# Earlier columns, later vectors, a later fourth block: the input stage of an encoder layer

## The chip, the cores and the metric

One core of one Trainium2 chip runs the whole layer in one launch. The metric is the device time in microseconds (us) of an execution; the time before is the median of three runs. Engines are named as in the profile: PE is TensorE, DVE VectorE, ACT ScalarE, POOL GpSimd, and SP the SyncE queue, from which nearly all transfers are issued.

## The reference

The input x has 2048 tokens of 1024 features. One layer is computed:

```python
h = rms_norm(x, norm_mix)
z = h @ w_in            # 1024 x 4352: q_A k_A v_A q_B k_B v_B gate_A gate_B
y_a = windowed_gqa(q_a, k_a, v_a, sink)     # window of 128 to both sides, ALiBi, a sink logit per head
y_b = neighborhood_attn(q_b, k_b, v_b, rpb) # 8 x 16 neighbourhood on a 32 x 64 grid
merged = sigmoid(g_a) * (y_a @ w_proj_a) + sigmoid(g_b) * (y_b @ w_proj_b)
x = x + merged @ w_out
x = x + relu(rms_norm(x) @ w_up)**2 @ w_down
return rms_norm(x)
```

The change lies in the product `h @ w_in`, in its first some 365 of 2631 us.

## The kernel before

**Precision.** Every fp32 operand of a matmul is split into a high part (a rounded copy, ScalarE, L293 or L176) and a low part (source minus high, VectorE, L294 or L177). One product is three matmuls: high x high, high x low, low x high (L297 to L299, and L200 to L202 in feature tiles).

**Blocks of x.** The tokens form four blocks of 512. Blocks 0 and 1 are loaded as four tiles of 128 tokens each (`x_tiles`, L365), normalised on VectorE, turned on PE (`turned`, L287, into a PSUM bank), and evicted with the gain `g_mix` by ScalarE (`scaled`, L517) and VectorE (`scaled_less`, L520). Blocks 2 and 3 are loaded later, normalised on ScalarE (`normalised`, L236), turned in 32 x 32 pieces on VectorE (`turned_out`, L260) and written to a tensor `h1d` in device memory (L268, 16 writes a block); `h_pages` (L678, split in L681 and L682) reads them back in the attention stage.

**Groups of columns ("quads").** For blocks 0 and 1, `in_quad` multiplies a 2 x 2 arrangement of halves (two halves of the features, two sets of columns; two blocks) in seven products instead of eight, in this order:

```python
ORDER = (1, 2, 5, 6, 7, 4, 3)
QUADS = [(O_KA, P), (O_QA, 256), (O_QB, 256), (O_KB, 256), (O_VB, 256)]
QUADS += [(O_GA + n * BT, 256) for n in range(4)]
```

Products 1 and 2 use only block 0 and the first set of columns of w_in: rows 0 to 511 for product 1, 512 to 1023 for product 2. The later ones use sums and differences of the halves, on the weights' side made by `in_left` (L290), on the tokens' side written out by hand between the `next(...)` calls. Results leave PSUM through L497 (ScalarE), L290, L439, L442/L443 and go to device memory by L463 and L474.

`row_half` (L527) loads one half of the rows with both sets of columns of a quad: 512 KB of K/V weights (`kvw`) for quad 0, 1 MB (`zraw`) for quad 1. Quads 0 and 1 run interleaved; the first two products of quad 2, whose first columns come by L571, are put ahead of quad 0's and 1's fifth. Each x tile of block 1 can be turned only when it is normalised (L222, L224, L227, L228, L557).

**Groups 2 to 8.** The loop over `q` runs quads 2 to 8, and loads each quad's weights one quad ahead. In q = 5 and q = 6 it also loads, normalises and turns blocks 2 and 3. In q = 7 the bias tables are made.

**Attention.** It starts when the quads end. The score matmuls are L758/L759, score reduction L760 (VectorE), softmax L763 to L771, transposes of the weights L777, products with v L782/L783. Between them "feature tiles" (`qk_tile`, `v_tile`, `gate_tile`) compute h @ w_in for blocks 2 and 3 from the h1d pages; their weight slices are loaded by L187 and split in L176/L177.

**What sets the order.** The program is traced in the order written. A scheduler in the language's tile layer then places every engine's instructions by its own timeline and by priorities, within the dependencies and the rings of buffers; each engine then runs its own list strictly in order. SP too: its issue of a transfer waits for what the transfer needs, and for the landing of the transfer eight earlier. `tc.issue_after(x)` keeps an instruction behind x.

Of the kernel before, what the change touches and what calls it, by code (L numbers as in the profile page):

```python
# [18 lines left out]
AH = 8  # L19
# [3 lines left out]
P = 128  # L23
KC = D // P
NB = 4
BT = 512
# [66 lines left out]
def encoder_layer(ctx, tc, x, norm_mix, w_in, b_gate, sink, rpb, w_pa, w_pb, w_out,  # L93
                  norm_mlp, w_up, w_down, norm_final, dist_a, mask_b, out):
    nc = tc.nc
    V, A, G, PE, SY = nc.vector, nc.scalar, nc.gpsimd, nc.tensor, nc.sync
# [9 lines left out]
    def pools(stack, side, tags, name):  # L106

        return {t: pool(f"{name}_{t}", side=side, stack=stack) for t in tags}
# [15 lines left out]
    def T(pl, shape, dt, tag, bufs):  # L124
        n_t[0] += 1
        pl = pl[tag] if isinstance(pl, dict) else pl
        return pl.tile(shape, dt, tag=tag, bufs=bufs, name=f"{tag}_{n_t[0]}")
# [5 lines left out]
    bg = cp.tile([P, 24], F32, name="bg")  # L133
    sink_t = cp.tile([P, AH], F32, name="sink_t")
# [11 lines left out]
    def bcast(ap1d, n):  # L146
        return bass.AP(ap1d.tensor, ap1d.offset, [[0, P], [1, n]])
# [9 lines left out]
    h1d = [dp.tile([D, BT], F32, name=f"h1d{b}") for b in range(2)]  # L157
# [53 lines left out]
    last_dma = [None]  # L211

    def load_tile(pl, tag, bufs, rows):
        t = T(pl, [P, D], F32, tag, bufs)
        last_dma[0] = SY.dma_start(t, rows).ins
        return t
# [14 lines left out]
    def rstd_of(pl, t, jp=None, mean=False):  # L231

        st = T(pl, [P, 4], F32, "st", 4)
        junk = T(pl if jp is None else jp, [P, 512], F32, "junk", 1)
        for n in range(2):
            A.activation(junk, t[:, n * 512 : (n + 1) * 512], AF.Square, scale=float(D) ** -0.5 if mean else 1.0,  # L236
                         accum_out=st[:, n : n + 1])
        r = st[:, 2 : 3]
        V.scalar_tensor_tensor(out=r, in0=st[:, 0:1], scalar=EPS if mean else D * EPS, in1=st[:, 1:2],
                               op0=ALU.add, op1=ALU.add)  # L240
        G.tensor_tensor(out=r, in0=r, in1=power, op=ALU.pow)
        return r

    def normalised(pl, tiles, jp=None, by_scalar=False):

        for t in tiles:
            if by_scalar:
                A.activation(t, t, AF.Copy, scale=rstd_of(pl, t, jp, True))
            else:
                V.tensor_scalar(t, t, rstd_of(pl, t, jp), float(D) ** 0.5, ALU.mult, ALU.mult)  # L250

    def turned_out(d, ht, tiles, g, gain=None, queue=None):

        hv = ht.rearrange("p (j t c) -> p t j c", j=8, t=4)
        for t in range(4):
            V.transpose(out=hv[:, t], in_=tiles[t][:, g * 256 : (g + 1) * 256].rearrange("p (j c) -> p j c", j=8))  # L260
        h3 = ht.rearrange("p (j x) -> p j x", j=8)
        if gain is not None:
            (step, n), _ = gain.ap
            gv = bass.AP(gain.tensor, gain.offset + 8 * g, [[step, n], [1, 8], [0, P]])
            V.tensor_tensor(out=h3, in0=h3, in1=gv, op=ALU.mult)
        dv = d.rearrange("(j i) (a x) -> a i j x", i=32, a=4)
        for a in range(4):
            (queue or SY).dma_start(dv[a][:, 8 * g : 8 * g + 8], h3[32 * a : 32 * a + 32])  # L268
# [20 lines left out]
    def add(eng, out, a, b, op=ALU.add):  # L289
        return eng.tensor_tensor(out=out, in0=a, in1=b, op=op).ins  # L290
# [10 lines left out]
    def halves(t):  # L301

        return t[:, 0:2], t[:, 2:4]

    def ring(stack, tag, shape, dt, bufs, side="right"):

        pl = pool(f"r_{tag}", side=side, stack=stack)
        return lambda: T(pl, shape, dt, tag, bufs)
# [22 lines left out]
    in_raw = ring(s_z, "zraw", PAGE, F32, 4, "left")  # L331
# [6 lines left out]
    in_e = ring(s_z, "ze", [P, 2, BT], F32, 2)  # L338
# [3 lines left out]
    kvw = ring(s_kv, "kvw", [P, 4, 256], F32, 2)  # L342
# [11 lines left out]
    def x_tiles(pl, b, bufs):  # L354
        out = []
        for t in range(4):
            xt = T(pl, [P, D], F32, "xin", bufs) if t < bufs else in_v2[0]()
            if b > 1:

                for a in range(4):  # L360
                    r = b * BT + a * P + t * 32
                    SY.dma_start(xt[32 * a : 32 * a + 32], xf[r : r + 32])
            else:
                r = b * BT + t * P
                last_dma[0] = SY.dma_start(xt, xf[r : r + P]).ins  # L365
            out.append(xt)
        return out
# [3 lines left out]
    def in_weights(c, w):  # L371

        return [row_half(c, w, p) for p in range(2)]

    def left_parts(src, w, eng):
        hl = in_whl()[:, :, :, 0:w]
        last_part[0] = split(src, hl[:, 0], hl[:, 1], eng)
        return hl
# [143 lines left out]
    QUADS = [(O_KA, P), (O_QA, 256), (O_QB, 256), (O_KB, 256), (O_VB, 256)]  # L522
    QUADS += [(O_GA + n * BT, 256) for n in range(4)]

    def row_half(c, w, p):
        t = kvw() if w == P else in_raw()
        SY.dma_start(t, w_in[0][p * BT : (p + 1) * BT, c : c + 2 * w].rearrange("(k p) f -> p k f", p=P))  # L527
        return t

    tiles = [x_tiles(xp, 0, 8), None]  # L530
    with nc.allow_non_contiguous_dma(reason="small per-feature vectors"):
        SY.dma_start(g_mix, norm_mix[0].rearrange("(k p) -> p k", p=P))
    ws0 = [row_half(*QUADS[0], p) for p in range(2)]
    ws1 = [row_half(*QUADS[1], 0)]
    tiles[1] = x_tiles(xp, 1, 8)
    ws1.append(row_half(*QUADS[1], 1))
    with tc.issue_after(last_dma[0]), nc.allow_non_contiguous_dma(reason="small per-feature vectors"):
        SY.dma_start(bg[:, 0:16], b_gate[0].rearrange("(k p) -> p k", p=P))
        SY.dma_start(sink_t, bcast(sink[0], AH))
    for t in tiles[0]:  # L540
        V.tensor_scalar(t, t, rstd_shared(xp, t), float(D) ** 0.5, ALU.mult, ALU.mult)
    right = {n: (in_page[n](), in_page[n]()) for n in (1, 2)}
# [25 lines left out]
    for p in range(2):  # L568
        t = T(xp, [P, D], F32, "xin", 8).rearrange("p (k c) -> p k c", k=4)
        c = QUADS[2][0]  # L570
        SY.dma_start(t, w_in[0][p * BT : (p + 1) * BT, c : c + 256].rearrange("(k p) f -> p k f", p=P))  # L571
        ops2.append(left_parts(t, 256, V))
        if p == 0:
            with tc.issue_after(last_part[0]):
                for o, h, l in zip(halves(t1), *map(halves, right[1])):
                    add(V, o, h.bitcast(F32), l.bitcast(F32))
        next(quad2)
    for n in (5, 3, 6):
        right[n] = (in_page[n](), in_page[n]())

# [41 lines left out]
    ws = in_weights(*QUADS[2])  # L622

    def bias_tables():
        rp = rpb[0]
        for n, (w, lo_rel) in enumerate(((24, -8), (32, -8), (24, -15))):
            tb = in_e()[0:BH].rearrange("h a b -> h (a b)")[:, 0 : T_ROWS * w]
            tb3 = tb.rearrange("h (r w) -> h r w", w=w)
            G.memset(tb, 0.0)
            ncol = min(w, 15 - lo_rel + 1)  # L630
            first = 15 + lo_rel
            SY.dma_start(tb3[:, T_RO - 7 : T_RO + 8, 0:ncol], rp[:, :, first : first + ncol])

            G.tensor_scalar(tb, tb, 8.0, 1.0, ALU.mult, ALU.mult)
            SY.dma_start(tabs[n], tb)

    for q in range(2, len(QUADS)):
        if q == 5:
            s_v.close()
            in_v2.pop()  # L640
            xp = pools(s_z, "right", ("xin", "st"), "x2")
        if q == 7:
            bias_tables()
        lf = list(in_left(ws, 256, (1, 2) if q == 2 else ()))
        if q + 1 < len(QUADS):
            ws = in_weights(*QUADS[q + 1])
        if q in (5, 6):

            b = q - 3
            xt = x_tiles(xp, b, 3)  # L650
            normalised(xp, xt, Junk(), by_scalar=True)
        ops2.extend(lf if q == 2 else ())
        for n, _ in enumerate(quad2 if q == 2 else in_quad(*QUADS[q], iter(lf), right)):
            if q in (5, 6) and 2 <= n < 6:
                turned_out(h1d[b - 2], in_e().rearrange("p k x -> p (k x)"), xt, n - 2)
    s_z.close()
    s_zp.close()

# [434 lines left out]
    def up_weights(q):  # L1093
        ws = []
        for p in range(2):
            w = up_rings["raw"]()
            SY.dma_start(w, w_up[0][p * BT : (p + 1) * BT, q * BT : (q + 1) * BT].rearrange("(k p) f -> p k f", p=P))
            ws.append(w)
        return ws
# [215 lines left out]
    for b in range(NB):  # L1315
# [43 lines left out]
        for t in range(4):  # L1359
            row0 = b * BT + t * P  # L1360
            xt = load_tile(p4x, "xr", 5, xf[row0 : row0 + P])
# [25 lines left out]
    for m in range(2):  # L1387
# [4 lines left out]
        ws = None  # L1392
        for q in range(8):
# [8 lines left out]
            if q < 7:  # L1402
                ws = up_weights(q + 1)
# [125 lines left out]
    for n in (1, 6, 2, 7, 5, 3, 4):  # L1529
        for group in ((range(8),) if n != 4 else (range(4), range(4, 8))):  # L1530
            part = None if n != 4 else group[0] // 4
# [63 lines left out]
```

## Time and profile before

| | us |
|---|---|
| Runs | 2630.62, 2633.14, 2633.35 (median 2633.14) |
| Profiled execution | 2632.52 |
| Its span on the core | 2630.6 |
| PE busy in it | 2588.6 (98%) |
| Mean granted PE clock | 0.997 of full |
| Quads end, first score matmul | 364.86 after the span's start |

A row of the timeline has the start and the length in us, the engine, the source line, the operation, what it writes and reads, and in brackets how long the engine sat idle before it and what ended that. A waits row names who waited, for which line of which engine, the us in total, how often and the longest. A groups row has busy us and mean ns of one, and the idle time before. A windows row has the stretch, its length, the busy us of PE, PEld (weight load), DVE, ACT and POOL, the granted clock, the DMA engines' share and GB/s. A row of the DMA view gives packets, MB and GB/s of its stretch.

### The profile page before, as it was taken

The numbers are of one execution on the slowest core, as the hardware profiler recorded it, in microseconds if no ns is written. First come the engines' busy times: TensorE is split into PE (matmuls) and PEld (weight loads), VectorE is DVE, ScalarE is ACT, GpSimd is POOL, SyncE is SP. The second block draws the span as 40 slices with busy tenths as digits, with TensorE's granted clock in tenths as the row PEclk, the third lists the DMA queues.
The fourth block names the chain that finished last, engine by engine and source line by source line (L and its number), as shares of the span: only waits on it lengthen the run. The fifth ranks groups of instructions, "written<-read, shape, count | busy, mean of one in ns | idle before, by whom it ended". The sixth has DMA issues, their size and how long they took to land.

```text
span 2630.6 us, 34485 instructions
## 1 busy us (share of the span) xinstructions
PE 2588.6 (98%) x12140; PEld 2154.3 (82%) x12140; DVE 1633.5 (62%) x2661; ACT 1230.6 (47%) x2245; POOL 349.9 (13%) x431
## 2 busy tenths in 40 slices
PE   7999999999999999999999999999999999999998
PEld 6888788778888888888887888888888888888887
DVE  8875666665544444756578677766656634554767
ACT  5334256666555555633334444644544322323444
POOL 1000014344555541000001000000000000000011
PEclk9999999999999999999999999999999999999999
DMA  5657476455876655954556755854428825444554
GB/s 168 204 164 200 133 238 167 113 155 145 241 218 180 189 149 163 311 183 152 170 184 200 244 203 198 306 183 155 145 107 295 302 101 183 146 146 168 184 190 170
DMA packets 352941, 490.28 MB, mean 186 GB/s; under 512 B 27752, under 2 KB 187624, under 8 KB 350592
## 3 DMA queue, kind: packets, MB, share of 16 engines
q1 hardware_dynamic: 345856, 471.30, 56.5%
q10 hardware_dynamic: 6912, 16.78, 1.8%
q8 instruction: 96, 1.57, 0.2%
q14 instruction: 77, 0.63, 0.1%
HBM read 328.53 MB, written 159.45 MB: 186 GB/s over the span
## 4 chain that ended last, share of the span: by engine, by line
PE 89%; DVE 5%; DMA 3%; ACT 2%; issue 1%; SPq 1%; POOL 0%; DVEq 0%; POOLq 0%; ACTq 0%
PE b L297 15%; PE b L299 15%; PE b L298 15%; PE mm L200 6%; PE mm L202 6%; PE mm L201 6%; PE zb L297 3%; PE zb L299 3%; PE zb L298 2%; PE pt L200 2%; PE pt L201 2%; PE pt L202 2%; PE av L960 2%; PE pt L948 2%; PE s L920 2%; PE pt L777 1%
## 5 line engine op out<-in xcount | busy, mean ns | idle before, releaser
L298 PE MATMUL b<-dwh,dah 128*128 128x512 f32 x896 | 349.0, 389 | 0.0
L299 PE MATMUL b<-dwh,dah 128*128 128x512 f32 x896 | 348.2, 390 | 0.0
L297 PE MATMUL b<-dwh,dah 128*128 128x512 f32 x896 | 339.9, 389 | 0.0
L293 ACT CAST dah<-da 128x1024 fp32r<-128x1024 f32 (+1 forms) x128 | 120.9, 945 | 367.7 <-PE b L299 242.7
L294 DVE TENSOR_TENSOR dah<-da,dah 128x1024 fp32r<-128x1024 f32 (+1 forms) x128 | 139.3, 1089 | 224.8 <-ACT dah L293 220.4
L297 PE MATMUL b<-ubh,uwhlb 128*128 128x512 f32 x592 | 230.9, 390 | 5.1 <-ACT uc L1255 3.2
L298 PE MATMUL b<-ubh,uwhlb 128*128 128x512 f32 x592 | 230.6, 390 | 0.0
L299 PE MATMUL b<-ubh,uwhlb 128*128 128x512 f32 x592 | 229.6, 390 | 0.0
L200 PE MATMUL mm<-hT,whl 128*128 128x512 f32 x544 | 218.3, 401 | 0.0
L202 PE MATMUL mm<-hT,whl 128*128 128x512 f32 x544 | 215.4, 396 | 0.0
L201 PE MATMUL mm<-hT,whl 128*128 128x512 f32 x544 | 214.1, 394 | 0.0
L297 PE MATMUL zb<-zh,zwhl 128*128 128x512 f32 x476 | 188.8, 398 | 8.8 <-DVE zc L290 3.7
L299 PEld LDWEIGHTS b<-dwh,dah 128*128 128x128 f32 x896 | 168.4, 188 | 34.8
L298 PEld LDWEIGHTS b<-dwh,dah 128*128 128x128 f32 x896 | 168.4, 188 | 34.7
L297 PEld LDWEIGHTS b<-dwh,dah 128*128 128x128 f32 x896 | 168.3, 188 | 34.7
L298 PE MATMUL zb<-zh,zwhl 128*128 128x512 f32 x476 | 187.7, 394 | 0.0
L299 PE MATMUL zb<-zh,zwhl 128*128 128x512 f32 x476 | 184.1, 394 | 0.3 <-DVE zwhl L294 0.3
L290 DVE TENSOR_TENSOR uc<-b,uc 128x512 f32<-128x512 f32 x160 | 109.1, 688 | 105.1 <-PE b L299 98.0
L1484 POOL TENSOR_TENSOR st<-st,power 128x1 f32<-128x1 f32 x16 | 13.5, 857 | 934.5 <-DVE st L1483 934.3
L297 PEld LDWEIGHTS b<-ubh,uwhlb 128*128 128x128 f32 x592 | 111.2, 188 | 30.0 <-ACT uc L1255 4.1
L298 PEld LDWEIGHTS b<-ubh,uwhlb 128*128 128x128 f32 x592 | 111.2, 188 | 23.0
L299 PEld LDWEIGHTS b<-ubh,uwhlb 128*128 128x128 f32 x592 | 111.2, 188 | 22.9
(248 smaller groups left out, 5902.7 us busy)
## 6 DMA issues: line engine op xcount, KB each, us to landing
at<-uc SPq DMA_DIRECT2D x224, 256.0 KB
da<-at SPq DMA_DIRECT2D x96, 512.0 KB
dw<-in_w_down_dram SPq DMA_DIRECT2D x160, 256.0 KB
uraw<-in_w_up_dram SPq DMA_DIRECT2D x32, 1024.0 KB
raw<-in_w_in_dram SPq DMA_DIRECT2D x34, 512.0 KB
zraw<-in_w_in_dram SPq DMA_DIRECT2D x16, 1024.0 KB
z<-zg SPq DMA_DIRECT2D x64, 256.0 KB
qa<-qs_a SPq DMA_DIRECT2D x32, 256.0 KB
```

The source lines that it names most:

```text
L200: PE.matmul(ps, lh, rh, start=first, stop=False)
L201: PE.matmul(ps, lh, rl, start=False, stop=False)
L202: PE.matmul(ps, ll, rh, start=False, stop=last)
L290: return eng.tensor_tensor(out=out, in0=a, in1=b, op=op).ins
L293: A.copy(hi, src)
L294: return eng.tensor_tensor(out=lo, in0=src, in1=hi.bitcast(F32), op=ALU.subtract).ins
L297: PE.matmul(ps, lh, rh, start=first, stop=False, skip_group_check=True)
L298: PE.matmul(ps, lh, rl, start=False, stop=False, skip_group_check=True)
L299: PE.matmul(ps, ll, rh, start=False, stop=last, skip_group_check=True)
L920: PE.matmul(ps[:, :n], q[:, i, :], kv[:, z, B_R0[i] // 4 : (B_R0[i] + B_NR[i]) // 4, 4 * B_C0[j] : 4 * (B_C0[j] + w)], start=z == 0, stop= ...
L948: PE.transpose(pt[:kp, at + (i - i0) * P : at + (i - i0 + 1) * P], s[i][:, rr : rr + kp], ident)
L960: last = PE.matmul(po[:, i0 * P : (i0 + ni) * P], v[:kp, c, :], src[:kp, o : o + ni * P], start=first, stop=(c == 7 and z == 1), skip_grou ...
```

## The change

- The loads of quads 0 and 1 are cut by columns. All four loads of the first set of columns (needed by products 1 and 2) are issued first, then block 1 of x, then the four loads of the second set, into the other halves of the same tiles. Rows of 512 B and 1 KB take the place of 1 KB and 2 KB.
- The small vectors `bg` (gate bias) and `sink_t` are issued behind quad 2's first products in the program's text.
- Block 3 of x (the fourth) is loaded in q = 7 instead of q = 6, and normalised and turned in q = 8, the last, around products 1 to 4 of the loop's count.

```diff
-    def row_half(c, w, p):
-        t = kvw() if w == P else in_raw()
-        SY.dma_start(t, w_in[0][p * BT : (p + 1) * BT, c : c + 2 * w].rearrange("(k p) f -> p k f", p=P))
+    def row_half(c, w, p, t=None, part=None):
+        if t is None:
+            t = kvw() if w == P else in_raw()
+        use = slice(0, 2 * w) if part is None else slice(part * w, part * w + w)
+        src = w_in[0][p * BT : (p + 1) * BT, c : c + 2 * w]
+        SY.dma_start(t[:, :, use], src[:, use].rearrange("(k p) f -> p k f", p=P))
         return t
...
-    ws0 = [row_half(*QUADS[0], p) for p in range(2)]
-    ws1 = [row_half(*QUADS[1], 0)]
+
+    ws0, ws1 = ([row_half(*QUADS[n], p, part=0) for p in range(2)] for n in range(2))
     tiles[1] = x_tiles(xp, 1, 8)
-    ws1.append(row_half(*QUADS[1], 1))
-    with tc.issue_after(last_dma[0]), nc.allow_non_contiguous_dma(reason="small per-feature vectors"):
-        SY.dma_start(bg[:, 0:16], b_gate[0].rearrange("(k p) -> p k", p=P))
-        SY.dma_start(sink_t, bcast(sink[0], AH))
...
         next(quad2)
+    for n, ws in ((0, ws0), (1, ws1)):
+        for p in range(2):
+            row_half(*QUADS[n], p, ws[p], 1)
+    with tc.issue_after(last_dma[0]), nc.allow_non_contiguous_dma(reason="small per-feature vectors"):
+        SY.dma_start(bg[:, 0:16], b_gate[0].rearrange("(k p) -> p k", p=P))
+        SY.dma_start(sink_t, bcast(sink[0], AH))
...
-        if q in (5, 6):
-
-            b = q - 3
+        if q in (5, 7):
+            b = 2 + q // 7
             xt = x_tiles(xp, b, 3)
+        if q in (5, 8):
             normalised(xp, xt, Junk(), by_scalar=True)
         ops2.extend(lf if q == 2 else ())
         for n, _ in enumerate(quad2 if q == 2 else in_quad(*QUADS[q], iter(lf), right)):
-            if q in (5, 6) and 2 <= n < 6:
-                turned_out(h1d[b - 2], in_e().rearrange("p k x -> p (k x)"), xt, n - 2)
+            if q == 5 and 2 <= n < 6 or q == 8 and 1 <= n < 5:
+                turned_out(h1d[b - 2], in_e().rearrange("p k x -> p (k x)"), xt, n - (2 if q == 5 else 1))
```

## The prediction

> **What bounds the kernel now.** I read the page first (busy time, chain), then PE's waits, then windows around the waits, then the timeline of the places that the change touches.
>
> ```profile
> span 2630.6 us, 34485 instructions
> PE 2588.6 (98%) x12140; PEld 2154.3 (82%) x12140; DVE 1633.5 (62%) x2661; ACT 1230.6 (47%) x2245; POOL 349.9 (13%) x431
> PE 89%; DVE 5%; DMA 3%; ACT 2%; issue 1%; SPq 1%; POOL 0%; DVEq 0%; POOLq 0%; ACTq 0%
> ...
> PE zb L297 <- DVE ze L443: 2.9, 1, 2.9
> PE zb L297 <- DVE zh L520: 2.0, 1, 2.0
> ...
> PE zb L297 <- DVE zc L290: 3.2, 2, 2.3
> ```
>
> TensorE (PE) is busy for 2588.6 of 2630.6 us and carries 89% of the chain, so only 42.0 us of idle time exist, and the change alters no matmul. The time moves by PE's idle time, and by its clock. Three stalls lie in the stages touched: one waits for L443 (2.9 us), one for L520 (2.0), one for L290 (2.3). The next rows show what follows each: window, its length, busy time of PE, PEld, DVE, ACT and POOL, granted clock, DMA share, GB/s.
>
> ```profile
> 24.44:27.85 3.41, 0.99 (x5) 0.49 (x3) 3.41 (x6) 1.23 (x3) 0.00 (x0) 1.00 0.89 291
> 27.85:31.27 3.42, 2.98 (x7) 2.41 (x8) 3.42 (x7) 0.61 (x1) 0.84 (x1) 0.50 0.51 115
> 55.16:58.57 3.41, 1.42 (x7) 0.90 (x6) 3.41 (x6) 2.00 (x2) 0.00 (x0) 1.00 0.00 0
> 58.57:61.98 3.41, 3.41 (x10) 2.65 (x9) 3.41 (x6) 0.00 (x0) 0.00 (x0) 0.50 0.34 67
> 270.20:273.61 3.41, 3.41 (x9) 2.65 (x9) 3.31 (x5) 0.00 (x0) 0.00 (x0) 0.50 0.94 330
> 300.00:340.00 40.00, 40.00 (x178) 33.17 (x177) 18.77 (x22) 11.98 (x15) 0.00 (x0) 1.00 0.25 92
> 1454.50:1457.90 3.40, 1.78 (x9) 1.25 (x8) 2.46 (x4) 2.02 (x3) 0.00 (x0) 1.00 0.97 337
> 1457.90:1461.30 3.40, 3.40 (x17) 2.82 (x16) 0.41 (x1) 1.23 (x2) 0.00 (x0) 1.00 0.94 356
> ```
>
> After a window in which PE was busy for 0.99 or 1.42 of 3.41 us, the next 3.41 us ran at clock 0.50; after one with 1.78 of 3.40 they did not. So each of the three stalls also costs about half of 3.41 us of full-speed work, call it 1.6. What could be gained at most is 2.9 + 2.0 + 2.3 + 3 x 1.6 = 12.0 us.
>
> **Part 1: columns of the first two products first, small vectors later.** The rows of the timeline: start, duration, engine, line.
>
> ```profile
> 12.76 10.25 SPq L539 DMA_DIRECT2D sink_t<-in_sink_dram  x1
> 23.52 1.23 DVE L290 TENSOR_TENSOR zS<-zraw,zraw 128x1024 f32<-128x1024 f32 x1 [2.12 <-DMA zraw<-in_w_in_dram]
> 24.66 0.68 DVE L224 CUSTOM_DVE_ANT_0 ze<-xin 128x512 f32<-128x512 f32 x1
> 25.04 0.39 PE L299 MATMUL zb<-zh,zwhl 128*128 128x512 f32 x1
> 25.46 0.60 ACT L442 ACTIVATE ze<-zb 128x512 fp32r<-128x512 f32 x1 [0.83 <-PE zb L299]
> 27.55 0.68 DVE L443 SCALAR_TENSOR_TENSOR ze<-zb,ze 128x512 fp32r<-128x512 f32 x1
> 28.29 0.79 PE L297 MATMUL zb<-zh,zwhl 128*128 128x512 f32 x1 [2.86 <-DVE ze L443]
> 39.27 1.80 PE L287 MATMUL zb<-ident,xin 128*128 128x128 f32 x15
> 57.10 0.74 DVE L520 SCALAR_TENSOR_TENSOR zh<-zb,g_mix,zh 128x512 fp32r<-128x512 f32 x1
> 57.99 0.47 PE L297 MATMUL zb<-zh,zwhl 128*128 128x512 f32 x1 [1.99 <-DVE zh L520]
> DMA packets 830, 1.12 MB, mean 374 GB/s; under 512 B 24, under 2 KB 539, under 8 KB 830
> DMA packets 702, 2.00 MB, mean 401 GB/s; under 512 B 49, under 2 KB 49, under 8 KB 702
> DMA packets 2072, 1.03 MB, mean 345 GB/s; under 512 B 125, under 2 KB 2048, under 8 KB 2072
> ```
>
> In the changed build the bytes are the same, but 1 MB of w_in moves in rows of 512 B instead of 1 KB and 2 MB in rows of 1 KB instead of 2 KB. The three DMA rows are stretches of 3, 5 and 3 us whose packets are mostly 1 KB and 2 KB, 4 KB, and 512 B. 1 MB at 345 instead of 374 GB/s costs about 0.2 us; 2 MB at 374 instead of some 388 (between 374 and 401) about 0.3. So the last piece lands 0.5 us later: zS (L290) can start at 24.0, not 23.52. The Trainium skill ("DMA: Bandwidth & Descriptors", Why small descriptors are slow) speaks against such a split: a fixed overhead of about 3 cycles a packet beside 32 B a cycle. By it I estimate 0.2 and 0.2 us, and a sum lower by 0.1; the 345 of the trace, 14% under 401, agrees with its 15 to 20% for 512 B.
>
> What is gained: the order on VectorE (DVE) becomes zS, L224, L443, while before an L294 and an L290 (start to start 1.14 us each, 23.52 to 24.66) stood between. zS 24.0 to 25.15, L224 to 25.8, then L443 waits for ACT's L442, which ends at 26.06 as before; with about 0.2 for the hand-over PE goes on at 27.0 instead of 28.29. Its last matmul before the gap still starts near 25.04, since block 0's x and turning are not moved. Gap 1.6 instead of 2.86; the window 24.44:27.85 is then busy for 1.8 of 3.41 us, just as the one that kept its clock. Minus 1.3, and probably minus 1.6.
>
> What is lost: PE's list is rearranged. Before, 15 of block 1's transposes ran together at 39.27. In the build, x tiles 2 and 3 of block 1 each come behind another 12 matmuls. From 27.0: 24 matmuls at 0.225 (178 in the 40.00 us from 300 to 340) and one bank wait of 0.7 give 33.1; 12 matmuls, 12 transposes (0.1 each), 12, 6, 12, 6 bring the last transposes of tile 3 to 43.7. VectorE must then do 16 of L520 (0.66 start to start), four 1024-wide operations (1.14) and three 512-wide ones (0.6): 16.9 us, from 44.9 to 61.8. Before, the last L520 began at 57.10. PE waits for that at its next-to-last step: between 43.7 and 62.0 it has 51 matmuls and 8 transposes, 12.4 us, so 6 us are idle against 1.99; but at 62.0 it stands 15 matmuls (3.4 us) further in its list than at 57.99 before. To a common point 60 matmuls behind 57.99: before 13.6 + 1.6 (half clock) gives 73.2; after, 45 matmuls give 72.2, and VectorE's ten operations ahead of the L290 that frees the bank (nine of 1.14, one of 0.6, then 0.7) hold it to 73.5, or 73.8 with a half clock. Part 1: plus 0.6; if the first stall still halves the clock, plus 2.2; if ScalarE and the scheduler's gaps are kinder, minus 1. Both ends stay in the range. Moving bg and sink costs nothing on PE: their landings are first needed in the attention stage, while sink's issue (10.25 us on SP) still stands ahead of quad 2's loads, as before; these land some 0.5 us later too, and PE needs what is made of them only at 37 us.
>
> **Part 2: block 3 loaded in group 7, turned in group 8.**
>
> ```profile
> 268.01 0.43 DVE L260 STREAM_TRANSPOSE ze<-xin 128x256 f32<-128x256 f32 x1
> 269.50 0.47 PE L297 MATMUL zb<-zh,zwhl 128*128 128x512 f32 x1 [2.32 <-DVE zc L290]
> 348.38 1.05 ACT L176 CAST whl<-raw 128x1024 fp32r<-128x1024 f32 x1 [1.72 <-DMA raw<-in_w_in_dram]
> 349.46 1.23 DVE L177 TENSOR_TENSOR whl<-raw,whl 128x1024 fp32r<-128x1024 f32 x1 [0.86 <-ACT whl L176]
> 364.86 0.28 PE L758 MATMUL s<-ka,qa 128*128 128x256 f32 x1
> 365.58 0.40 PE L200 MATMUL mm<-hT,whl 128*128 128x512 f32 x1
> 365.06 0.69 DVE L290 TENSOR_TENSOR zc<-zb,zc 128x512 f32<-128x512 f32 x1 [1.83 <-PE zb L299]
> L760 DVE CUSTOM_DVE_ANT_0 sa<-s,biasa,sink_t 128x384 f32<-128x384 f32 x26 | 15.2, 606 | 2.4 <-PE s L759 2.3
> L760 DVE CUSTOM_DVE_ANT_0 sa<-s,biasa,sink_t 128x256 f32<-128x256 f32 x8 | 3.7, 480 | 4.4 <-PE s L759 3.8 <-PE pt L777 0.4
> L682 DVE SCALAR_TENSOR_TENSOR hT<-raw,g_mix,hT 128x512 fp32r<-128x512 f32 x8 | 5.6, 747 | 1.8 <-ACT hT L681 1.8
> 366.00:390.00 24.00, 24.00 (x124) 20.65 (x124) 13.39 (x45) 12.95 (x39) 11.61 (x20) 1.00 0.85 254
> PE s L758 <- DVE sta L760: 1.9, 3, 1.1
> PE av L783 <- DVE pl L781: 1.4, 3, 0.8
> ```
>
> Gone: in group 6 the turning (L260) stands ahead of the L290 for which PE waits 2.32 us, and the half clock behind it: minus 3.9. In group 8 the same 16 transposes (0.4 each) fall into a stretch where VectorE is less than half busy (18.77 of 40.00 us from 300 to 340); 0 to 1.5, taken 0.5. Loading and ScalarE's normalising of the four x tiles go along into groups 7 and 8, where ScalarE has 11.98 of 40.00 us and the DMA engines a share of 0.25: nothing, as long as the rows are there a group ahead.
>
> New: the quads end at T (364.86 before). There the weight slice of the first feature tile had long been split (L176 at 348.38, L177 at 349.46), so feature-tile matmuls (L200) at once filled the time in which the softmax of the first attention tiles ran, and PE had 24.00 busy of 24.00 us. In the build SP gets 16 writes of block 3 to h1d ahead of the reads of block 2 (L678) and of the first slice; each of SP's issues waits for the landing of the one eight earlier. The slice's load is issued only near T - 0.4, its cast on ScalarE stands behind the first softmax (to about T + 8.6), and L177 on VectorE stands behind 12 score reductions (L760). Price on VectorE from T: last L290 0.8 (365.06 to 365.7), four L760 of 256 columns 2.4 (0.48 and the reading of the accumulator, taken as 0.59), eight of 384 columns at 0.61, 4.9, small ones 0.6, two L682 at 0.66 back to back, 1.3, L177 1.1, hand-over 0.2: PE's first product with the low half starts at T + 11.3. Until then it has 12 pairs of score matmuls (three pairs of 256 columns fill 364.86 to 365.58, 0.24 a pair, so 0.36 for 384 columns: 4 x 0.24 + 8 x 0.36 = 3.8), two feature-tile matmuls (0.5) and six transposes (0.6): 4.9. Idle 6.4; with 0.7 a reduction, small operations between them, 7.1; taken 6.7. At 40% busy the clock halves as in the rows above: plus 1.6 behind it. Block 3's rows are read through the same ring still later: 0 to 2, taken 0.7.
>
> Part 2: -3.9 + 0.5 + 6.7 + 1.6 + 0.7 = +5.6. Behind that, PE's list is the same as before.
>
> **Sum.** +0.6 + 5.6 = +6.2 on the profiled execution's 2632.52 us (span 2630.6, 1.92 around it) is 2638.7. That execution lies 0.6 below the median of 2633.14, so on the median I forecast 2639. Own range: part 1 from -1 to +2.2, part 2 from +3 (0 in group 8, 6.0 idle, half a half clock, 0) to +7.5: 2635 to 2643.
>
> **The rivals.**
> - Front-loading is repaid. Place: the attention stage from 366 to 620, where PE waits for L760 and L781, 1.9 + 1.4 us. While PE idles at T, twelve reductions are already done, so these waits may vanish: 2639 - 3.3, about 2636, no change. It decides if VectorE keeps that lead for over 100 us; against it speaks that the list behind the first slice is unchanged and each wait is local to a pair.
> - Both stages work as drawn: the slice is not late (its load and cast go out ahead of the softmax), and the second stall of part 1 is hidden: -3.9 - 2.9 - 1 = 2625. The positions in the lists speak against it: 12 L760 ahead of one L177.
> - Worse: the turning in group 8 stalls PE as it did in group 6 (+3.4 more, 3.9 instead of 0.5) and the first stall halves the clock (+1.6): 2644. For it: VectorE is in order, and its L260 waits for a ring of two tiles.
> - A gap under 3 us costs only itself: PE's idle time at T comes in pieces of under 3 us, so no half clock follows, and 1.6 goes from the sum: 2637.4, no change. Against it: the three rows at 0.50 above, behind gaps of 2.86, 1.99 and 2.32 us. The Trainium skill has it as a rule ("TensorE: Matmul & The Clock Gate", Why this matters for your kernels: no idle gaps over some 3 us); this trace disagrees.
>
> **How the numbers follow.** Forecast 0.57, the rule on gaps 0.03, worse 0.16, repaid 0.11, as drawn 0.13. 0.2% (5.3 us) is about what a measurement can tell here: faster is below 2627.9, slower above 2638.4. Of the forecast's own range some 0.65 lies above 2638.4: 0.37, with worse 0.53; its rest, the rule on gaps and repaid make same, 0.34; faster is 0.13. For 8 in 10 I leave out "as drawn" and little else: from "repaid" at the forecast's lower end (2635 - 3.3), less 1.4 (half of what the runs before differ by), 2630, to "worse" with block 3's reading at its upper bound, 2646.
>
> **What would show it.** Right: PE's wait at L443 near 1.6 us; a wait of several us at 50 to 62 us for L520; no wait near 267; in the first 12 us after the quads PE busy near 40%, with waits for L767 (L760 moved) and then for L177, and clock 0.50 behind. Wrong: PE busy over 80% there, or a gap near 27 as long as before.

## The result, and the profile after

| | before | after |
|---|---|---|
| Median of six runs, us | 2632.71 | 2649.18 (2647.78 to 2652.19) |
| Ratio after/before | | 1.0064, 95% interval 1.0054 to 1.0074 |
| First profiled execution, us (span) | 2632.52 (2630.6) | 2652.19 (2650.3) |
| Second profiled execution of the changed kernel, us (span) | | 2648.44 (2646.5) |

The change makes the kernel slower by 16.5 us by the medians, 0.64% by the ratio. Slower was the likeliest sign in the prediction, but the size is outside its range (2630 to 2646).

The first profile happens to be of the longest of the six runs: it has a stall of 2.4 us and a half clock at 118 us that no other profile here shows. So a second profile of the same kernel (**after_again** below) is read here. First its page: span, busy time.

```profile
span 2646.5 us, 34476 instructions
PE 2595.1 (98%) x12140; PEld 2156.6 (81%) x12140; DVE 1634.7 (62%) x2661; ACT 1229.8 (46%) x2245; POOL 358.9 (14%) x431
```

The matmuls are the same 12140. PE's idle time is 51.4 us (2646.5 - 2595.1) against 42.0, and its busy time grew by 6.5 us (2588.6 to 2595.1), in part because of the half clock: matmuls start every 0.43 us there (381 to 383 us) instead of every 0.23 (362 us). PE's waits from 0 to 130 us, then from 360 to 450:

```profile
...
PE zb L297 <- DVE zh L520: 3.1, 1, 3.1
PE zb L297 <- DVE ze L443: 1.5, 1, 1.5
PE zb L297 <- DVE ze L439: 1.2, 1, 1.2
PE zb L297 <- ACT zh L293: 1.0, 1, 1.0
...
PE s L765 <- DVE zc L290: 5.5, 1, 5.5
PE pt L784 <- POOL sa L778: 2.1, 1, 2.1
PE av L789 <- DVE ya L794: 1.9, 1, 1.9
PE mm L200 <- ACT whl L176: 1.1, 1, 1.1
```

The wait for L443 shrank from 2.9 to 1.5, as forecast, and the group-6 wait for L290 is gone (from 255 to 300 us PE waits for nothing). The big new one is the first score matmul (L765, L758 before): 5.5 us. The row names L290, but that ended at 368.0, and q's transfer says more: SP issued it at 359.66 and its last packet landed at 368.71; PE went on at 368.80. In the kernel before, the same transfer took as long (issued at 354.09, landed at 363.03), but that was 1.8 us before PE needed it. The windows show what the clock did (columns as in the prediction):

```profile
59.67:63.08 3.41, 1.18 (x4) 0.48 (x3) 3.41 (x6) 2.12 (x3) 0.00 (x0) 1.00 0.00 0
63.08:66.49 3.41, 1.55 (x4) 1.30 (x5) 3.41 (x5) 1.99 (x2) 0.00 (x0) 0.50 0.02 5
66.49:69.91 3.42, 3.42 (x10) 2.68 (x9) 3.42 (x4) 0.00 (x0) 0.00 (x0) 0.50 0.00 0
363.46:366.87 3.41, 0.00 (x0) 0.00 (x0) 3.15 (x5) 1.63 (x3) 2.50 (x4) 1.00 1.04 330
366.87:370.28 3.41, 1.48 (x7) 1.38 (x7) 1.72 (x5) 0.00 (x0) 0.00 (x0) 0.50 1.14 330
370.28:373.70 3.42, 3.42 (x12) 3.42 (x12) 3.20 (x14) 1.94 (x9) 0.00 (x0) 0.50 1.10 370
373.70:377.11 3.41, 2.36 (x10) 1.28 (x9) 3.41 (x12) 3.41 (x10) 0.00 (x0) 1.00 1.13 232
377.11:380.52 3.41, 1.23 (x7) 0.59 (x7) 2.52 (x8) 2.09 (x8) 3.02 (x4) 1.00 1.14 238
380.52:383.94 3.42, 3.42 (x10) 2.75 (x10) 1.36 (x1) 2.44 (x6) 3.42 (x6) 0.50 1.15 319
438.55:441.96 3.41, 1.49 (x7) 0.87 (x6) 3.41 (x7) 3.39 (x11) 1.56 (x1) 1.00 1.00 331
441.96:445.38 3.42, 3.42 (x13) 3.08 (x13) 2.35 (x9) 1.79 (x7) 0.90 (x2) 0.50 0.93 276
```

Of these windows, each with PE busy for 0.00 to 1.55 of 3.41 us is followed by one at 0.50, and the one with 2.36 by one at 1.00. The half clock is paid three times behind the quads, where the prediction counted it once. Why q came late is in SP's rows of the timeline:

```profile
341.50 7.99 SPq L268 DMA_DIRECT2D h1d<-ze  x11
349.54 0.48 SPq L745 DMA_DIRECT2D ka<-ks_a  x1
351.31 1.36 SPq L268 DMA_DIRECT2D h1d<-ze  x3
353.78 0.53 SPq L268 DMA_DIRECT2D h1d<-ze  x1
354.35 1.50 SPq L685 DMA_DIRECT2D raw<-h1d  x1
359.66 2.71 SPq L758 DMA_DIRECT2D qa<-qs_a  x3
367.72 0.43 SPq L187 DMA_DIRECT2D raw<-in_w_in_dram  x1
```

The same in the kernel before:

```profile
327.54 6.93 SPq L678 DMA_DIRECT2D raw<-h1d  x3
340.25 0.38 SPq L187 DMA_DIRECT2D raw<-in_w_in_dram  x1
354.09 2.36 SPq L751 DMA_DIRECT2D qa<-qs_a  x3
```

The reads of h1d begin 27 us later (354.35 against 327.54), the first weight slice 27 us later, and q 5.6 us later, all now within some 15 us. The DMA engines have a share of 1.06 while q is on its way (359.66 to 368.71), but in the kernel before it was 1.03 (354.09 to 363.03): q is late because it is issued late, not because its transfer takes longer.

### The profile page after: what moved, and what is told of

Read it like the earlier page. It is cut to its first block, busy times and chain, and to the rows that moved or that the text cites. A ratio compares the mean times of both kernels' runs of the same rounds, so it can differ in the third digit from the quotient of the medians.

```text
span 2650.3 us, 34476 instructions
## 1 busy us (share of the span) xinstructions
PE 2597.0 (98%) x12140; PEld 2158.0 (81%) x12140; DVE 1636.5 (62%) x2661; ACT 1230.4 (46%) x2245; POOL 352.4 (13%) x431
## 3 DMA queue, kind: packets, MB, share of 16 engines
q8 instruction: 96, 1.57, 0.2%
## 4 chain that ended last, share of the span: by engine, by line
PE 89%; DVE 4%; DMA 3%; issue 1%; ACT 1%; POOL 1%; SPq 0%; POOLq 0%; DVEq 0%; ACTq 0%
PE b L299 15%; PE b L297 15%; PE b L298 15%; PE mm L202 5%; PE mm L200 5%; PE mm L201 5%; PE zb L297 3%; PE zb L299 3%; PE zb L298 3%; PE pt L200 2%; PE pt L201 2%; PE pt L202 2%; PE av L967 2%; PE pt L955 2%; PE s L927 2%; DMA braw<-tab 1%
## 5 line engine op out<-in xcount | busy, mean ns | idle before, releaser
L293 ACT CAST dah<-da 128x1024 fp32r<-128x1024 f32 (+1 forms) x128 | 120.9, 945 | 368.3 <-PE b L299 246.2
L294 DVE TENSOR_TENSOR dah<-da,dah 128x1024 fp32r<-128x1024 f32 (+1 forms) x128 | 139.4, 1089 | 223.7 <-ACT dah L293 223.6
L290 DVE TENSOR_TENSOR uc<-b,uc 128x512 f32<-128x512 f32 x160 | 109.1, 689 | 104.1 <-PE b L299 97.1
```

The source lines that it names most:

```text
L293: A.copy(hi, src)
L294: return eng.tensor_tensor(out=lo, in0=src, in1=hi.bitcast(F32), op=ALU.subtract).ins
```

## The experiments

One number recurs below. PE runs 12140 matmuls in every kernel, so the start of the n-th one (counted from 0) can be compared with that of the n-th before. "Input" is that difference at the 1531st (364.6 us before, the end of the quads), "transition" is what is added up to the 1900th (436.3 us before). For the changed kernel they are -1.7 and +16.2. Both come from single profiles, the ratios from several runs beside runs of the kernel before (medians 2632.56 to 2633.91). A single profile has its luck: p1_vec runs the same lists on PE and SP as the kernel before and stands at -1.5, because two of its stalls left the clock at 1.00. So inputs that differ by 1 or 2 us are not told apart here.

| kernel | median, us | ratio to before, interval | input | transition |
|---|---|---|---|---|
| after_again | 2648.9 | 1.0059 (1.0044 to 1.0074) | -1.7 | +16.2 |
| p1_only | 2637.33 | 1.002 (1.001 to 1.0029) | +3.0 | 0.0 |
| p1_vec | 2632.24 | 1.0 (0.9991 to 1.0009) | -1.5 | 0.0 |
| p1_prio200b | 2639.41 | 1.0025 (1.0015 to 1.0035) | +7.1 | 0.0 |
| p2_only | 2647.61 | 1.0055 (1.004 to 1.007) | -6.3 | +15.1 |
| p12_actq | 2651.65 | 1.0071 (1.0056 to 1.0086) | -0.2 | +12.4 |
| p12_q67 | 2635.9 | 1.0011 (1.0002 to 1.002) | +2.3 | 0.0 |
| nowrite8 | 2645.47 | 1.0049 (1.0035 to 1.0062) | -1.4 | +10.8 |
| hold8 | 2638.9 | 1.0022 (1.0012 to 1.0032) | +3.4 | +2.8 |
| hold8lateb | 2637.6 | 1.0023 (1.0014 to 1.0033) | +1.7 | +3.1 |
| hold346 | 2645.3 | 1.0046 (1.0031 to 1.0061) | +1.6 | +3.0 |
| hold352 | 2644.28 | 1.0051 (1.0034 to 1.0067) | -1.2 | +10.8 |
| p2_q67 | 2632.48 | 0.9999 (0.999 to 1.0008) | +2.4 | 0.0 |
| turn7b | 2630.03 | 0.9992 (0.9983 to 1.0) | -2.7 | 0.0 |

**The two parts alone.** p1_only is the kernel before with the first two pieces of the diff, p2_only with the last one.

> Part 1 alone: columns of the first two products first, small vectors later; block 3 loaded and turned in group 6 as before. In the changed kernel's trace PE stands 2.85 us later than before at the common point near 74 us and 6.3 us later behind a new stall near 118 us; the quads' end and the transition to attention are then as before. Theory (the transition is the larger loss, part 1 the smaller): about 2632.7 + 6.3 = 2639, with the wait of 2.3 us near 267 still there and PE busy in the first 12 us of attention. Rival (part 1 is what costs, through the later order of everything): 2645 or more.

> Part 2 alone: block 3 loaded in group 7, normalised and turned in group 8; the first loads as before. Theory (SP's queue at the transition): group 6 gives back 4.7 us and group 8 about 1, then the first score matmul waits some 5 us for q's rows, and the whole transition costs 16.4: 2632.7 - 5.7 + 16.4 = 2643, up to 2646 with what is lost near 700 us. Rival (it needs both parts together): under 2637.

Part 1 costs 2.9 us in the profile and some 5 by the median, part 2 some 15. The transition is part 2's alone. Of part 2's 15 us, some 6 came up at 1439 us, far from the change, where the scheduler had put a few instructions otherwise; the changed kernel has nothing of it, so it is not followed here.

**The writes through another queue (p12_actq).**

```diff
-                turned_out(h1d[b - 2], ..., n - (2 if q == 5 else 1))
+                turned_out(h1d[b - 2], ..., n - (2 if q == 5 else 1), queue=A if q == 8 else None)
```

> The whole change, but the 16 writes of block 3 to h1d are issued from ScalarE's queue instead of SP's; the same bytes at nearly the same time. Theory (they stand ahead of q's, k's and the first weight slice's loads on SP): those loads go out as early as before, the wait of 5.7 us before the first score matmul goes, and most of the 16.4 us of the transition: 2633 to 2637. Rival (the DMA engines are full there, a share of 1.02 to 1.11, so the rows land late from whichever queue): the wait stays within 1.5 us of 5.7 and the time near 2649.

The kernel did not get faster, though the 16 writes were off SP's own list. Locally it gained a little: the transition fell from 16.2 to 12.4 us and the wait for the first score matmul from 5.5 to 4.0, but some 6 us came up near 1440 us, at the same far place as in p2_only. SP's waits from 335 to 375 us in this kernel:

```profile
...
SPq L746 <- DMA h1d<-ze: 5.9, 1, 5.9
SPq L729 <- DVE ze L260: 3.8, 1, 3.8
SPq L686 <- DMA h1d<-ze: 3.1, 3, 2.2
```

SP still waits for the landing of writes that ScalarE's queue issued (5.9 and 3.1 us): "the transfer eight earlier" counts over both queues. The second row pointed to something else: SP waits 3.8 us at L729, the load of `dist`, for the turning (L260). Nothing in the source ties the two together; by the addresses of the built kernel `dist` lies in the memory of one of block 3's x tiles, and the first tile that h1d is read into lies where its fourth x tile was.

**Not in the last group (p12_q67).** The whole change, but block 3 is loaded in group 6 and turned in group 7.

```diff
-        if q in (5, 7):
-            b = 2 + q // 7
+        if q in (5, 6):
+            b = q - 3
...
-        if q in (5, 8):
+        if q in (5, 7):
```

> The whole change, but block 3 is loaded in group 6 and normalised and turned in group 7: one group on instead of two. Theory: the writes to h1d leave SP some 38 us before the quads end, so the transition runs as before (PE at over 95% in its first 24 us), while the stall of group 6 stays away: 2649.2 - 16.4 or so, 2632 to 2635. Rival (the stall of group 6 only moves to group 7, where the bias tables are made on the same queue): 2636 to 2639.

The transition is back to 0.0. The input of +2.3 is not part 1 alone: PE is 3.4 us late ahead of group 6, which gives 4.7 back, and group 7 then costs 3.6, since normalising and turning bring a stall along there (the rival, in part). But the 16 us at the transition come from doing the turning in the last group, not from moving it.

**Writes against memory.** Two causes remained, and they were taken apart from both sides. nowrite8 turns block 3 in group 8 but does not write it (`turned_out` writes to those of `d` and `also` that are given).

```diff
-                turned_out(h1d[b - 2], ...)
+                turned_out(h1d[0] if q == 5 else None, ..., also=h1d[1] if q == 5 else None)
```

> The whole change, but in group 8 block 3 is only turned; its 16 writes to h1d are left out (block 2's rows are written twice in group 5 instead, so block 3's results are those of block 2). Loads, VectorE work and the memory held by the x tiles stay as in the change. Theory (SP's queue: the 16 writes stand ahead of q's and the slice's loads, each behind the landing eight earlier): the first score matmul no longer waits some 5 us, the idle time from 365 to 383 us falls from 11 to under 3, and the time to about 2638, the remainder being part 1 (+2.5 to +7). Rival (memory: reads of h1d and the weight slice reuse the memory of x tiles that live until the last turning of group 8): the writes do not matter, the same stalls stay, 2648. Between: both, with some 2643.

hold8, and then hold8lateb, take p12_q67, which loses nothing, and only read block 3's x tiles once more in group 8.

```diff
+            if q == 8 and n == 4:
+                he = in_e()[:, 0, 0:P]
+                for t in range(4):
+                    V.transpose(out=he[0:32, 32 * t : 32 * t + 32], in_=xt[t][0:32, 0:32])
```

> The whole change, but block 3 is loaded in group 6 and turned and written in group 7 (measured before at 2635.9), and four small 32x32 reads of its x tiles are put into group 8, results unused, so that the tiles' memory is held as long as in the change while no write and no turning is late. Theory (SP's queue): nothing comes back, 2636 +- 1.5, no wait for q at the transition. Rival (memory held late): the reads of h1d and with them q's and the slice's loads come late again, idle from 365 to 383 of 5 us or more, 2642 to 2648.

> Again the whole change with block 3 loaded in group 6 and turned and written in group 7, and the four small 32x32 reads of its x tiles in group 8, now two products later, about where the change's last turning stands (some 350 us instead of 343). No write and no turning is late. Theory (memory: the rings that h1d and the first weight slices are read into reuse the x tiles' memory, and the later it comes free the later those loads): the first slice is issued after 357 us, the transition costs 8 to 12 us, and the time is 2644 to 2648, although nothing but a few small reads was added to a kernel of 2636. Rival (SP's 16 writes and the late turning cost it all): 2639 or less, as with the earlier hold.

Without the writes 5.4 us of 16.2 are gone, and 10.8 stay. The hold cost only 3; but hold8lateb (n == 6) did not hold longer: the scheduler drew the four reads forward to 342 us again. So the next two tie them to a piece of the weights that is made late.

```diff
+                late = lf[-1][0:32, 0, 0, 0:32].bitcast(F32)      # hold346: lf[-2]
+                for t in range(4):
+                    add(V, he[0:32, 32 * t : 32 * t + 32], xt[t][0:32, 0:32], late)
```

> The whole change with block 3 loaded in group 6 and turned and written in group 7, and in group 8 four small 32x32 additions that read block 3's x tiles and a weight piece which is made late, results unused, so that the tiles' memory comes free at about 346 us, as in the kernel without writes (where that was 346.3, and the transition cost 10.8). Theory (memory: reads of h1d and the first slices go into the tiles' memory): transition 5 to 11 us, first slice issued after 354, time 2640 to 2646. Rival (the turning's own work on VectorE and the ring it shares): 3 us as with the hold to 342, 2638.

> The same with a weight piece made later still, so that the tiles' memory comes free at about 352 us, as in the change (352.9). Theory (memory): transition 11 to 17 us, 2647 to 2653, with a wait for q or for the first slice of 3 to 6 us, although no write and no turning is late. Rival (writes on SP and the turning's work): under 5, at most 2640. If it falls between, the writes' own share is what is missing to 16.5.

hold352 loses 10.8 us in the transition although no write and no turning is late. SP's waits from 335 to 375 us, then PE's from 360 to 450, in hold352:

```profile
...
SPq L690 <- DVE ze L290: 7.8, 1, 7.8
SPq L763 <- DMA raw<-h1d: 2.7, 1, 2.7
...
PE pt L789 <- DVE pl L793: 1.8, 1, 1.8
PE mm L202 <- DVE whl L177: 1.6, 1, 1.6
PE s L770 <- DMA qa<-qs_a: 1.5, 1, 1.5
PE mm L200 <- ACT whl L176: 1.2, 1, 1.2
```

The first row is the mechanism in one line: SP, about to issue a read of h1d (L690), waits 7.8 us for the four small additions (L290 on `ze`) that do nothing but keep the old tiles alive; q and the slice queue behind. So memory held late is enough for two thirds of the loss, and the rest comes with the writes: nowrite8, which has all but them, loses the same 10.8. The holding changed SP's list too: the first slice stands behind q in hold352 (issued at 363.28), ahead of k and q in the kernel before (340.25). How much is the wait itself and how much this order, which the scheduler chose, no run separates.

hold346 lost only 3.0 us in the transition, as its rival said, although its memory came free later than in nowrite8 (347.6 against 346.3 us). How much a given lateness costs also hangs on when PE gets there. The first slice's cast in the timeline of nowrite8, and then in that of hold346:

```profile
366.18 1.04 ACT L176 CAST whl<-raw 128x1024 fp32r<-128x1024 f32 x1 [4.49 <-DMA raw<-in_w_in_dram]
```

```profile
365.37 1.05 ACT L176 CAST whl<-raw 128x1024 fp32r<-128x1024 f32 x1 [1.73 <-DMA raw<-in_w_in_dram]
```

Only 0.8 us lie between them, and yet the one loses 10.8 us and the other 3.0: at the end of the quads PE is 3.0 us further ahead in nowrite8 (-1.4 against +1.6), has nothing else to do, waits 2.5 us for that cast and then runs at half clock; a wait of 1.8 us at 433 us has a half clock behind it too. These four (2.5, 1.7, 1.8, 1.7) make up the 7.7 us between the two, so the lead is more than given back. hold346's time by the median is worse than its transition, by a wait of 4.8 us at 1435 us, again far off in the rearranged part. Not settled is how much of nowrite8's 10.8 is the memory and how much the turning's work.

**A second profile of the changed kernel.**

> The changed kernel a second time. If the stall at 118 us (2.4 us and a half clock, ScalarE's L442 behind writes that stand behind other transfers) belongs to the change, it is there again and the profile comes to 2650 to 2652; if it is a matter of one execution, the profile comes to about 2647.5 to 2648.5 with under 1 us there, and part 1 and the transition alone make the difference.

The stall at 118 us was not there: it belongs to one execution.

**Part 1 in pieces.** p1_vec issues only the small vectors late.

> The kernel before with only the small vectors issued late, columns loaded as before. Theory (part 1's loss of 2.5 to 3 us and its gain of 1.3 both come from the column split): no change, 2632.6 +- 0.6. Rival (sink's issue, 10 us on SP, now stands in front of other loads, or no longer delays block 1): 2631 or 2635.

No change. SP's order is in fact the same as before, since the scheduler issued `bg` and `sink_t` ahead of quad 2's loads anyway (sink at 12.36 us, before 12.76). Part 1 is the columns. p1_prio200b raises the priority of block 1's turning in p1_only.

```diff
+    with tc.high_priority(offset=200):
         for n, t in enumerate(tiles[1]):
...
+        with tc.high_priority(offset=200):
             turned(ps, tiles[1], k)
```

> Part 1 alone, with a higher priority for block 1's normalising (L543 on) and transposes: in PE's list the last transposes of block 1 come 12 matmuls (2.7 us) earlier. Theory (part 1 loses because block 1 is turned late and VectorE's 16 L520 behind it end late): the stalls at 61 to 64 us shrink from 2.5 us by 1 to 2.5, and part 1 goes from +2.9 to between 0 and +1.5, 2633 to 2634.5. Rival (VectorE's work up to that point is the bound, whatever the order on PE): no change, +2.5 to +3, 2635 to 2637.

My theory fell: with the last transposes 12 matmuls earlier in PE's list, part 1 got no better (2639.41 against 2637.33, with intervals that overlap; 2.9 of the +7.1 came up in group 6, where this profile ran two windows at half clock). VectorE's list suggests why. The windows of p1_only, and one row of its timeline:

```profile
40.00:44.00 4.00, 4.00 (x23) 3.32 (x22) 1.64 (x3) 0.58 (x1) 0.00 (x0) 1.00 0.64 205
44.00:48.00 4.00, 4.00 (x23) 3.40 (x22) 2.37 (x3) 3.93 (x7) 0.00 (x0) 1.00 0.00 0
48.00:52.00 4.00, 3.26 (x19) 2.54 (x17) 4.00 (x6) 4.00 (x8) 0.00 (x0) 1.00 0.00 0
60.00:64.00 4.00, 1.52 (x6) 0.65 (x6) 4.00 (x7) 3.89 (x5) 0.00 (x0) 1.00 0.00 0
```

```profile
45.63 1.22 DVE L294 TENSOR_TENSOR zwhl<-zS,zwhl 128x1024 fp32r<-128x1024 f32 x1 [3.92 <-ACT zwhl L293]
```

From 48 us VectorE (third busy time) is full until past 76 us, here as before, and the stalls of PE only say when its work is done. What differs is the time ahead of that: VectorE sits idle for 3.92 us behind ScalarE's cast L293, which itself waits in its list for a product of PE (L497, 44.07). In p1_prio200b it was 3.09 and 1.59, together 4.7 us. That the idle time is the cause is read from these three traces (before: 1.9 us between 36 and 44); it was not tried by itself.

**What can be kept.** p2_q67 (before, with block 3 loaded in group 6, normalised and turned in group 7), and then turn7b, where only the turning moves:

```diff
-            if q in (5, 6) and 2 <= n < 6:
+            if q == 5 and 2 <= n < 6 or q == 7 and 1 <= n < 5:
-                turned_out(..., n - 2)
+                turned_out(..., n - (2 if q == 5 else 1))
```

> The kernel before with block 3 loaded in group 6 as before but normalised and turned in group 7; nothing of part 1. If the gains and losses of the parts add up: group 6 gives back about 3.9 to 4.7 us, group 7 has a stall of 1.4 and maybe a half clock behind it (1.6), so 2632.6 - 4.3 + 2 = about 2630.5 (2629 to 2632). Rival (the scheduler's far rearrangement, as in the change's part 2 alone, where 6 us came up at 1440 us): 2634 to 2637.

> The kernel before with one thing moved: block 3 is loaded and normalised in group 6 as before, and only its turning and its writes go one group on, into group 7. Where normalising and turning both went to group 7, the group-6 stall went (4 us) and a stall of 2.7 us with a half clock came in group 7, behind ScalarE (L236 and L248 stand ahead of the casts L293 there). Theory (ScalarE's normalising causes the group-7 stall, VectorE's turning the group-6 one): neither stall here, 2632.6 - 4 = about 2628.5 (2627.5 to 2630). Rival (the turning brings its stall along): 2631 to 2634.

p2_q67 exchanges the stall of group 6 for one in group 7, where the normalising puts ScalarE's casts back. turn7b leaves the normalising in its place. PE's waits from 255 to 300 us in turn7b:

```profile
PE zb L297 <- ACT zc L497: 0.9, 1, 0.9
PE zb L297 <- DVE zc L290: 0.7, 1, 0.7
```

In place of 2.3 us and a half clock there are 0.9 and 0.7 with none. At 2630.03 against 2632.69 it is the only version clearly below the kernel before, by 2.7 us, and the interval ends at 1.0: a small gain, just short of the theory's 2627.5 to 2630 and at the edge of what five rounds can show.

## Why the prediction was wrong

- **Part 1, first stall** (1.6 instead of 2.86, the clock kept): right. Measured 1.5, at 1.00.
- **Part 1, second stall.** Foreseen: PE idle at 50 to 62 us behind L520, and +0.6 at a common point, at 73.8 us. In kind right, in size not: in p1_only that point comes at 75.8, +2.5. The step that failed is the stretch "16.9 us, from 44.9 to 61.8": VectorE, which had been idle for 3.92 us behind L293, began it at 45.63, and five 1024-wide operations (L294, L290) stood among the 16 L520 instead of the four counted, so the last L520 ended at 63.73. These 1.9 us are the difference. The bound of +2.2 was too low too.
- **Group 6**: -3.9 forecast; the wait and the half clock are gone, and by p2_only's matmuls between the 1060th and the 1180th the gain is 4.7. **Group 8**: no stall from turning (0.5 forecast).
- **The transition**, the step that sank the forecast. The first half of it held: the writes stood ahead, and in the four windows from 363.46 to 377.11 PE was busy for 7.3 of 13.65 us, two thirds of that at 0.50. The size did not: 9.0 us forecast (6.7 idle, 1.6 half clock, 0.7), 16.2 measured.
  - The idle time was reckoned from a T at which the score matmuls start at once ("12 pairs of score matmuls ... 3.8"): the 16 writes were set against the slice alone, though q's loads are on the same queue. q was late by 5.5 us before anything else, and nowrite8 shows it: without the writes that wait is gone, and 5.4 us with it.
  - The slice, forecast for T - 0.4, came at T + 4.4 (367.72 against the quads' end at 363.33). But of the waits named, for L767 and then L177, neither came: PE waited 1.1 us for the slice's cast (L176) and 2.1 for the first softmax (L778, on POOL). That is 3.2 us where 6.7 were forecast. The idle time of 8.7 in all is thus near 6.7 by luck, with q in the place of VectorE's reductions.
  - The half clock came to 5.8 us instead of 1.6: some 2.4 in the windows from 366.87 to 373.70, 1.7 at 380.52, 1.7 at 441.96. A wait of 1.9 us at 439 us, not in the sum at all, makes the rest.
- **What was not seen at all**: that a tile's last reader sets when another tile's load into the same memory may start. I took the h1d reads to be late because the writes stand ahead of them; hold352 shows them late with no write there.
- **The rivals.** "Worse" (2644) came nearest, but by neither of its conditions: group 8 did not stall, and the first stall kept its clock. "As drawn" failed on the slice, which was late. "Repaid" is refuted: behind the 1900th matmul the difference does not shrink (+14.5 there, +15.8 at the end). The rule on gaps has the trace against it again: a gap of 2.1 us at 377 and one of 1.9 us at 439 had a window at 0.50 behind them. The Trainium skill ("TensorE: Matmul & The Clock Gate", Why this matters for your kernels) asks for no idle gaps over some 3 us; here shorter ones cost the clock as well.

## What to carry to other kernels

A load has three things that can hold it: its place in the queue, the landings it must wait for, and the last reader of whatever used its memory before; for the last one look at the addresses, not the source. Work that is moved to the end of a stage can move all three for the first loads of the next stage, and where these loads set the pace, an engine that arrives earlier only waits longer. When an engine is full for tens of us, as VectorE from 48 to 76 us here, look at when that stretch begins and what stands in it before changing the order of what feeds it.

## What the runs showed of the hardware

The half clock hangs on how the gaps fall into windows of 3.41 us, not on their length alone. (But for the last one, at each kernel's end, every stretch at half clock in these profiles lasts 3.41 us or twice that.) The same wait of 1.4 us in group 7, first in p2_q67 and then in p12_q67, each with the window behind it:

```profile
291.15:294.56 3.41, 1.57 (x6) 0.66 (x6) 3.34 (x5) 1.60 (x3) 0.00 (x0) 1.00 0.20 75
294.56:297.98 3.42, 3.42 (x10) 2.65 (x9) 3.35 (x4) 0.00 (x0) 0.00 (x0) 0.50 0.02 7
```

```profile
291.37:294.78 3.41, 2.12 (x9) 1.19 (x7) 2.96 (x3) 3.24 (x5) 0.00 (x0) 1.00 0.14 53
294.78:298.19 3.41, 2.86 (x11) 2.09 (x12) 3.34 (x4) 0.00 (x0) 0.00 (x0) 1.00 0.22 82
```

In p2_q67 the wait and another of 0.4 us fall into one window, in p12_q67 into two: with 1.57 us busy the window is followed by 0.50, with 2.12 it is not. A wait of 3.01 us for L443 in p1_vec, over two windows, cost no clock, where the 2.86 us of the kernel before did. There is no sharp limit by these busy times: a window of p1_only with 1.48 us (269.52 to 272.94) is followed by 1.00, one of hold346 with 1.88 (1424.91 to 1428.32) by 0.51.

And with the DMA engines full, a transfer of 256 KB took 9 us from issue to landing (q: 359.66 to 368.71, in the kernel before 354.09 to 363.03), so a load that is issued 5.6 us late has no slack left to hide it.
